# Grouped-query attention on one core: two q heads cast singly, and the copies of the keys' other half moved behind q's transposes

## The chip, the core and the metric

The kernel runs on one core of a Trainium2 chip. The core has a matrix engine (TensorE, PE in the rows), a vector engine (VectorE, DVE), an activation engine (ScalarE, ACT), a general engine (GpSimd, POOL) and an engine that issues transfers (SyncE, SP). Each takes its own list of instructions in order, and they wait for one another by semaphores. Transfers (DMAs) run on 16 DMA engines of the core. The metric is the device time of one execution in microseconds (us); the time shown of the kernel before is the median of three runs.

## The reference

```python
batch, n_q_heads, n_kv_heads, seq, head_dim = (8, 8, 2, 1024, 64)
...
for g in range(n_kv_heads):
    q_group = q[:, q_start:q_end, :, :].copy()
    k_group = k[:, g:g + 1, :, :].copy()
    v_group = v[:, g:g + 1, :, :].copy()
    scores = scale * np.matmul(q_group, k_group.transpose(0, 1, 3, 2))
    scores_max = np.max(scores, axis=-1, keepdims=True)
    attn = np.exp(scores - scores_max)
    attn = attn / (np.sum(attn, axis=-1, keepdims=True) + 1e-08)
    output[:, q_start:q_end, :, :] = np.matmul(attn, v_group)
```

Inputs and output are float32. There are 8 batches of 8 q heads, 64 heads in all (0 to 63 below), and 16 key and value tiles, each shared by four consecutive q heads.

## The kernel before, in words

**Tiles.** The scores of one head are computed transposed, in eight tiles: a score tile holds 128 keys against 512 queries, twice, for the two halves of the queries. One tile is a pair of matmuls (L400), which read `qt` (a head of q, turned) and `kt` (a key tile, turned). There are 512 score tiles. Each is turned into weights by ScalarE (`pt`, an exponential, L411) or by VectorE and GpSimd together (`ye` and `zz`, L422, L431, L448, L457, L463: an exponential made from the bits of a float). PE then multiplies the weights by the values `va` (L491) into `ops`, with a column of ones for the sums; VectorE takes the reciprocal (L560) and scales the result (L571) into `ost`, which SyncE stores (L378).

**Loads of q and k.** Head 0 and key tile 0 are turned on PE at the start. Every other head goes this way: GpSimd issues a DMA that casts float32 to bfloat16 into a buffer in DRAM (`qd`, L174, called from `cast_q`), most of them two heads at a time; SyncE then issues a DMA that turns a head on its way into `qt` (L243, `turn_q`). A key tile goes the same way by `kd` and `kt` (L233, `turn_k`). Such a turned tile holds the even sequence rows in partitions 0 to 63 and the odd ones in 64 to 127. Two more DMAs (`copy_k`) write the other half of `kt`, the same data with the partition halves exchanged, for the score tiles 4 to 7 of each head:

```python
nc.sync.dma_start(out=t[D : 2 * D, 1, :], in_=t[0:D, 0, :])
nc.sync.dma_start(out=t[0:D, 1, :], in_=t[D : 2 * D, 0, :])
```

Both read what the transpose of the key tile wrote, so the first of them waits on SyncE until that has landed, and everything behind it on SyncE's list waits too. The rows call them L237 and L238.

**The order.** The string `ORDER` sets the order of the whole program by hand; each letter appends instructions to the lists of their engines. `A` is a score tile for ScalarE, `a` to `g` one for VectorE, `x` and `p` are their exponentials, `V` some weighted sums. `X4`, `X6`, `X8` cast heads of q (`q10` and on do the same later), `Y` and `k` cast key tiles, `Z` and `v` values; `T` turns the next head, `K` the next key tile, `C` makes its two copies, `U` loads values, `S` stores a head, `G` is a product on GpSimd. A cast by `X`, `Y` or `Z` is also made to wait for the score tile that stands last before it in the string (L348). In the rows of the order below, `qd_171` and its like are the cast heads; the number only tells one buffer from another.

Of the kernel before, what the change touches and what calls it, by code (L numbers as in the profile page):

```python
# [25 lines left out]
VVVG0,108nxd2A0TpVSVVxVVVVA1zd2xA0TG1,148pVVVVVxVVVVA1Crnd2xA0pVSVVVVxVG0,36VVVA1zk2e2xA0pVVVG1,47VV
xVVVVVA1zq16d2xA0t3VVVVVG2,115rVxVpVA1VVVVxVVVnA0d2m2xVSVG1,71VpA1TVVxVVVVA0t2e2xG1,78pA1VVVVVxUVVA0
rze2TxVVG2,107VKpA1VVxVVVVVnA0A2xzq18VSVVVVVt3Ve1xA0G2,84pTVVVVVxVVVA2rzd1xA0G3,172pVVVVVxVVVVVA2nCe
1xA0pVVVVVVxVVVA2v2rt3A1xVVVm2VVVVVVVxe0A2G1,192pVVVxVVVVTA1ne0xA2pVSVVVVxVVVVA1rt2e0q20xA2pVVVG1,47
VVxVVVVA1m1G0,106e0nxA2pVSVVVVxUVVVA1ze0xA2G1,78pVVVVVxVVVA1rze0xA2G2,72pVVVVxVVVTA1t3e0xVG1,192VpA2  # L30
VVVxVVA1ne0xVVpVSA2VVVxVVVrA1m1q22A0t2xVVVVVt1VTVVVxVVG0,32nd2A1zVSVxVVG1,71A0pVVVxVVKVVA1zd2xA0G2,7
8rpVVVVVxVVVVA1zd2xA0G3,75pTVVVVVxVVVA1nG2,18A2xVzVk3VSVVVVVt4Vxd0A1G3,191rpTVCVVVxVVVVA2ne0xA1pVSVV
VVVxVVVA2m2q24A0xVVVVVVVrVt2xVVVVA1G3,30nd2xA0m3G1,71pSTVVVVVxVVVA1t3d2xA0G1,79pVVVVVxVVA1rzA2xVVVm2
VVVVVG1,106nd0xUA1pVVVVVxVVVVA2m1q26A0xVVKVt2VVTVVVVxVt1d1A2G0,72pVVxVVVA0VVzxVv3VVVA1Tzd2xA0G2,184r
pVVVVVxVVVVA1nd2xA0pSVVVVCVxVVVVrA1t2d2xA0G1,71pVVVVVxVVVVzA1q28A2xVzVVVVVG3,114nd0xA1pVSVVVxVVVVA2r
Tm3A0xG2,30VnVVVVVt3Se1xA2G2,71pVVVVVxVVVA0m2e1xA2G1,78pTVVVVVxVUVVA0rt2d1xA2G1,178pVVVVxVVVVA0nTd1x
A2pSVVVVVxVVVA0q30zA1xVzVVVVVVVrG2,106nxd2A0pVVSVVxVVVVA1t3d2xA0KG2,71pVVVVVxVVVA1ze2xA0G3,79pVVVVVx
VVVA1rTzA2k4xVVt4VVVVVVG3,115xne0A1pVSVVxVVA2VVrCVxm3Vq32VVVA0m2A1xVVVVVVVTVVG1,106nxe2A0pVSVVVxVVVV
VA1Tt3d2xA0G1,78pVVVVVVxVVVA1rt2A2xVVVm1VVVVG0,107nd0xA1pVVVVVxVVVVA2t1d0xVG0,78VpTA1VVVxVUVVA2rzA0x
VVq34zVVVVVVnxe1G2,71A2pVSVVVxVVKVVA0G1,10rne1G1,98xA2pVVSVVVxVVVVA0t2v4e1xA2pTVVG1,47VVVxVVVA0ze1xA  # L40
2G2,78pVVVVVxVVVA0rm2G1,106e1CnxA2pTVSVVVxVVVVA0t2e1xA2G1,71pVVVVVxVVVA0m1q36A1zxVVVVVG1,122VrVnVxd2
A0pSVVVVxVVVVA1t2e2xA0G1,71pVVVVVxVVVVA1ze2xA0G2,63pVVVVVVxVUVVVTzA1e2xG2,78rA0pVVVVVVxVVVA1t3A2xVzV
VVVTVVVG3,114ne0xA1pVSVVVxVVVKVA2rm3A0q38xzVVVVVVt4e1xA2G3,225pVVVVVxVVVTA0nd1xA2rpSVVVVVxVVVVA0ne1x
A2m3G2,71SpVVVCVVxVVVVA0t3k5A1xVVm2VVVVe2xG1,78A0rpVVVVVxVVVVA1zq40A2xVVzVVVVVVG3,106ne0xA1pVTVVVVxV
VVVA2t4e0xA1G3,72pVVVVVxVVVVVA2rG2,105ne0xA1pSVVVVVVxVUVVVm2A2e0xA1G1,78pVVVVVVxVVVA2rTt3d0xVVVG1,71
pA1VVVxVVVVzA2q42A0xVzVKVVVVG3,107nd1xA2pTVSVVVVxVVVA0t4d1xA2G2,78rpVTVVVVxVVVA0t3v5d1xA2pVG2,82VVVV
xVVVA0nA1CxVm2VVSVVTVzVd2xA0G2,191rpVVVVVxVVVVA1nd2xA0pSVVVVVxVVVVt3A1q44e2xm2A0G1,70VpVVVVxVVVVA1t2
e2xA0G1,78pVVVVVxVVVVA1rm1e2xA0G0,228pVVVVVxVVUVVTA1ne2xA0rSpVVVVVxVVVA1nA2xVm0VVSt1VVTVVVVxt0VA0A1q
46zVxVVVzVVVVVVxVzd2A0G2,114rpVVxVVVVKA1VVxnVVVVA2m2Sd0xA1G1,71pVVVVVxVVVVt2A2Te0xG1,114rA1pVVVVVxVV
VVA2nA0xVzk6VVVVVVVzCe1xA2G3,71pVVVVVxVVVVVA0Trq48t3e1xA2pVVG2,90VVVVxVVVVA0nA1xVm1VVSVVVd2xA0G2,71T  # L50
pVVVVxVVVVA1m2e2xG0,78A0rpVVVVVxVVVA1t2e2xG0,107A0pVVVVVxVUVVA1nA2xVzVVSVVVVt2Ve0xA1G1,71rpVVVVxVVVV
VA2q50ze0xA1pTVVG1,204VVVxVVVA2ne0xA1rpSVVVVVxVVVA2nA0xVzv6VSVVVVt3e1xA2KG2,52pVVVVVxVVVVA0ze1xA2G2,
71pVVVVVxVVVVA0t3Td1xVG2,185VrVpA2VVxVVVVTA0ne1xA2pSVVVVCVxVVVA0q52zA1xVVzVVVVVVrVG3,106nxd2A0pVSVVV
xVVVVA1t4d2xA0G3,71pVVVVVxVVVVTA1m3A2xrVt3VVVVVVG2,108Vne0xA1pVSVVVVxVVVVA2ze0xA1G3,78pVVVVVxVVVUVA2
rzA0q54xVVVVm4VTVG3,108Vne1xKA2pVVVVxVVVVA0t4d1xA2G3,71pVVVVVxVVVTzA0e1xG4,77rA2pVVVVVxVVVA0nG3,24A1
xzVk7VSVVVCVt5d2xA0G4,71pVVTVVxVVVVA1m4q56A2xVVVrVt4Ve0xG3,202A1pVVVVVxVVVVA2nd0xA1pSVVVVVxVVVA2rm3e
0G2,106nxVVA1pSVVVxVVVVA2t3e0xA1G2,71pVVVVVUxVA2m2xze0A1TTt3xA2G2,71pVVVxVVVVVA1zq58A0xVVm3VVVVVVe2x
G2,199A1rKpVVVVVxVVVVA0nd2xA1pSVVVVVVxVVVA0Tm2v7A2t3xVVVVVt2VVVxd1G1,200A0rpVVVVxVVVVVA2nCe1xA0pSVVV
VVVxVVVVzA2Te1xG2,56rA0pVVVVVVxVVG1,45VA2nA1xVzq60VVSVVVVVt3e0xA2G2,78pVVVVVxVVVVVA1rm2e0xA2G1,184pV
VVVVxVVVA1ne0xA2pSVTVVVxVUVVA1t2A0xVVm1VVVVzVe2xA1G1,194rpVVVVxVVVVA0ne2xA1pVVVTVVxVVVVm1q62A0t2d2xA  # L60
1G0,75pVVVVVVxVVVA0rt1d2xA1G0,181pVVKVVVxVVVA0ne2xA1pSVVVVxVVVA0zq63A2TxVVzVVVVVVt2xe1A0G1,199rpVVVx
VVVVVA2ne1xCA0pVSVVVVxVVVVVrA2m1e1G0,106nxA0VVpVVSVVVxVVVVA2Tt1d1xA0G0,71pVVVVVVxVVVVA2TzA1xVVm1VVVV
VrVt1Vxe0A2G0,185pVVVVxVVVVVA1ne0xA2pSVVVVVVxVVVUVA1zd0xA2G1,71rpVVVVVVxVVVVA1zA0xVVt2VVVVVVG1,106nd
2xA1pVSVVVVxVVVVA0ze2xA1G2,71pVVVVVxVVVA0m2A2rxVt2VVVVVG1,112Vnxe1A0pSVVVVxVVVVVA2zd1xA0G2,114rpVVVV
VVVxVVVA2nA1xVm2VVSzVVVVVVxVt3VVA0A2m1xVVVVVVVVVm2xVVVA1A0xVVrVt2VVVVVxVnVVA2rt1A1xVVVzVVVVVVxTnVVVV
# [30 lines left out]
def kernel(  # L96
# [76 lines left out]
    def cast(src, t):  # L173
        return nc.gpsimd.dma_start(  # L174
            out=t.rearrange("(a x) d -> a (x d)", a=128),
            in_=src.rearrange("(a x) d -> a (x d)", a=128),
        )
# [429 lines left out]
```

## Time and profile before

| what | value |
|---|---|
| median of 3 runs | 356.24 us (356.08 to 357.02) |
| the profiled execution's own time | 354.45 us |
| its span, first to last instruction | 352.7 us |
| PE, DVE, ACT, POOL busy, share of the span | 97%, 97%, 96%, 82% |
| chain that ended last | PE 58%, ACT 25%, DVE 7%, DMA 5% |
| mean granted clock of PE | 0.990 |

Rows of a timeline read: start, length, engine, line, operation, written tile `<-` read tiles, shape, count, and in brackets the idle time of the engine just before and what ended it. `SPq` is SyncE's list; its rows give the time that the issue of a DMA took, not the transfer. The time to landing runs from the issue to the end of the transfer. The clock column of the windows table is the share of full speed that was granted to PE.

### The profile page before, as it was taken

Reading aid. Unit: us, or ns where it says so; the run is one execution under the profiler, and the core shown is the slowest. Engines: PE = TensorE matmul, PEld = TensorE weight load, DVE = VectorE, ACT = ScalarE, POOL = GpSimd, SP = SyncE. Lnnn points to the kernel's source line nnn. Section 1 sums busy time; section 2 is a strip of 40 time slices with the busy share of each in tenths; the row PEclk is TensorE's granted clock in tenths of the full one; section 3 lists DMA queues with packets and bytes.
Section 4 is the critical chain, followed back from the end, with each engine's and each line's share of the span. In section 5 each row is a group of like instructions: output and inputs, shape, how many; then the busy total and the mean of one; then the engine's idle time right before and its main releaser. Section 6 shows DMA issues by size and latency. Waiting matters only on the chain.

```text
span 352.7 us, 14190 instructions
## 1 busy us (share of the span) xinstructions
PE 341.2 (97%) x6268; PEld 225.7 (64%) x6268; DVE 342.3 (97%) x518; ACT 340.1 (96%) x370; POOL 287.9 (82%) x235
## 2 busy tenths in 40 slices
PE   7879999999999999999999999999999999999995
PEld 3445665666666666666666676766665666676774
DVE  5979999999999999999999999999999999999996
ACT  6959999999999999999999999999999999999994
POOL 3447989999988999998999989899998989987000
PEclk9979999999999999999999999999999999999999
DMA  6986677675787588677668979576876653623123
GB/s 149 141 160 122 127 134 160 137 121 110 134 159 126 126 153 128 122 149 148 121 121 122 165 153 136 98 162 113 156 138 134 140 122 80 134 63 88 51 82 103
DMA packets 96574, 44.84 MB, mean 127 GB/s; under 512 B 61168, under 2 KB 95344, under 8 KB 95728
## 3 DMA queue, kind: packets, MB, share of 16 engines
q1 hardware_dynamic: 94128, 31.34, 40.3%
q0 software_dynamic: 2096, 12.19, 24.0%
q8 instruction: 49, 0.80, 1.0%
q10 hardware_dynamic: 288, 0.39, 0.3%
q14 instruction: 13, 0.11, 0.1%
HBM read 27.13 MB, written 28.97 MB: 159 GB/s over the span
## 4 chain that ended last, share of the span: by engine, by line
PE 58%; ACT 25%; DVE 7%; DMA 5%; issue 2%; SPq 1%; POOL 0%; DVEq 0%
PE ops L491 32%; PE sp L400 25%; ACT pt L411 25%; DVE ye L422 3%; DMA kt<-kd 2%; DMA qt<-qd 1%; DMA vs<-in_v_dram 1%; DMA kd<-in_k_dram 1%; DVE ye L463 1%; DVE ost L571 1%; DVE zz L431 1%; PE sp L529 1%; DVE zz L457 0%; SPq L238 0%; DVE rec L560 0%
## 5 line engine op out<-in xcount | busy, mean ns | idle before, releaser
L411 ACT ACTIVATE pt<-sp 128x1024 bf16<-128x1024 f32 x366 | 337.5, 1049 | 5.0 <-PE sp L400 4.9
L448 POOL TENSOR_TENSOR zz<-ye,zz 128x568 bf16<-128x568 bf16 (+29 forms) x126 | 248.4, 1973 | 27.8 <-DVE rec L560 8.7
L422 DVE TENSOR_SCALAR ye<-sp 128x1024 uint16<-128x1024 f32 x146 | 177.3, 1214 | 2.4 <-PE sp L400 2.0
L400 PE MATMUL sp<-qt,kt 64*128 64x512 bf16 x1024 | 167.2, 384 | 6.2 <-ACT pt L411 2.6
L491 PE MATMUL ops<-va,pt 128*128 128x65 bf16 x2832 | 161.9, 195 | 0.0
L491 PEld LDWEIGHTS <-pt 128*128 128x128 bf16 x2832 | 121.4, 98 | 31.4 <-issue 31.4
L491 PE MATMUL ops<-va,zz 128*128 128x65 bf16 x1136 | 123.7, 194 | 0.0
L491 PE MATMUL ops<-va,ye 128*128 128x65 bf16 x1104 | 119.5, 194 | 0.0
L491 PEld LDWEIGHTS <-ye 128*128 128x128 bf16 x1104 | 83.8, 98 | 15.7 <-issue 14.8
L491 PEld LDWEIGHTS <-zz 128*128 128x128 bf16 x1136 | 86.4, 98 | 9.2 <-issue 8.9
L400 PEld LDWEIGHTS <-kt 64*128 64x128 bf16 x1024 | 51.2, 93 | 61.7 <-issue 38.1
L431 DVE TENSOR_SCALAR zz<-ye 128x2048 uint16<-128x2048 uint16 (+1 forms) x77 | 51.9, 686 | 0.1
L463 DVE TENSOR_SCALAR ye<-ye 128x2048 uint16<-128x2048 uint16 (+1 forms) x77 | 49.9, 655 | 0.0
L571 DVE TENSOR_TENSOR ost<-ops,rec 128x448 f32<-128x448 f32 (+2 forms) x73 | 44.5, 610 | 0.3
L457 DVE TENSOR_TENSOR zz<-ye,zz 128x2048 bf16<-128x2048 bf16 (+31 forms) x54 | 33.5, 625 | 0.0
L174 POOL DMA_DIRECT2D qd<-in_q_dram x33 | 23.3, 706 | 5.5 <-PE sp L400 4.7
L560 DVE RECIPROCAL rec<-ops 128x7 f32<-128x7 f32 (+2 forms) x73 | 14.4, 197 | 0.8 <-PE ops L491 0.8
L443 POOL MEMSET tick<- 128x1 bf16 x52 | 9.7, 186 | 0.0
L174 POOL DMA_DIRECT2D kd<-in_k_dram x8 | 5.8, 719 | 0.1
L174 POOL DMA_DIRECT2D vd<-in_v_dram x8 | 5.6, 701 | 0.0
L269 PE MATMUL ops<-warm 128*128 128x512 bf16 (+1 forms) x12 | 3.6, 448 | 1.2 <-DVE warm L168 1.2
L529 PEld LDWEIGHTS <-pt 128*128 128x128 bf16 x96 | 3.4, 98 | 1.2 <-issue 1.2
(37 smaller groups left out, 26.1 us busy)
## 6 DMA issues: line engine op xcount, KB each, us to landing
out_dram<-ost SPq DMA_DIRECT2D x63, 256.0 KB, 3.2
qd<-in_q_dram POOLq DMA_DIRECT2D x29, 256.0 KB, 4.5
kt<-kt SPq DMA_DIRECT2D x30, 64.0 KB, 4.5
va<-vd SPq DMA_DIRECT2D x30, 64.0 KB, 3.1
kd<-in_k_dram POOLq DMA_DIRECT2D x7, 256.0 KB, 4.5
vd<-in_v_dram POOLq DMA_DIRECT2D x7, 256.0 KB, 5.2
qt<-qd SPq DMA_TRANSPOSE x63, 4.2
qd<-in_q_dram POOLq DMA_DIRECT2D x5, 128.0 KB, 3.9
```

What stands on the lines that cost most here:

```text
L174: return nc.gpsimd.dma_start(out=t.rearrange("(a x) d -> a (x d)", a=128), in_=src.rearrange("(a x) d -> a (x d)", a=128),)
L400: now = nc.tensor.matmul(sps[x][:, hf, :], lhsT=t[lo : lo + D, c // NH, ci % NH * 128 : (ci % NH + 1) * 128], rhs=qt[j][lo : lo + D, 0, :] ...
L411: exps.append(nc.scalar.activation(out=p, in_=where_s[(j, c)], func=AF.Exp, scale=scale))
L422: vec = nc.vector.tensor_scalar(out=ye[:, i, :, :], in0=where_s[(j, c)], scalar1=EXP_A, scalar2=EXP_B, op0=ALU.mult, op1=ALU.add,)
L431: vec = nc.vector.tensor_scalar(out=ch.tiles(zz), in0=ch.tiles(ye), scalar1=0x7F, scalar2=0x3F00, op0=ALU.bitwise_and, op1=ALU.bitwise_or,)
L443: tock = nc.gpsimd.memset(tick, 0.0) if any(old) else None
L448: gps = nc.gpsimd.tensor_tensor(out=z, in0=flat(ch.tiles(ye))[:, ch.cols : ch.cols + w], in1=z, op=ALU.mult)
L457: vec = nc.vector.tensor_tensor(out=z, in0=flat(ch.tiles(ye))[:, 0 : ch.cols], in1=z, op=ALU.mult)
L463: vec = nc.vector.tensor_scalar(out=ch.tiles(ye), in0=ch.tiles(ye), scalar1=0x7F80, scalar2=None, op0=ALU.bitwise_and,)
L491: ended[job] = nc.tensor.matmul(ops[g % 2][:, lo : lo + D + 1], lhsT=p[:, par, qs * 128 : (qs + 1) * 128], rhs=va[(b * G + h // HPG) % NVA ...
L560: vec = nc.vector.reciprocal(out=to, in_=sums)
L571: vec = nc.vector.tensor_tensor(out=to, in0=src, in1=by, op=ALU.mult)
```

## The change

In `cast_q`, heads are cast in pairs from head 6 on instead of head 4 on. In `ORDER`, `X4` stands earlier and casts head 4 alone, `X5` is new and casts head 5 alone at about the place where `X6` stood, and `X6` and `X8` (heads 6 and 7, heads 8 and 9) stand later. The first `C` moves behind three `T`, and each of the other fourteen `C` also stands later, behind other instructions of SyncE's list. Some `T` move by a few letters. No instruction of PE, ScalarE or VectorE changes its place.

```diff
-A0IX3TY1a1xA2pxA0za1xKA2pE0E2TxFA0m0E3xA1za2t1E5X4FxpFA0E1xm0A1X6E6zxb2t1A0pE7E4xA1Crzxb2nG0,78A0pxA
-1TTY2m1xb2A0G0,50pxA1X8t1Z1xA2zb0VVVt1VxVVG0,78VpA1TVVxVVVVrA2zc0G1,101xnVVpA1SVVxVVVVVKA2rm1A0xG0,3
...
+A0IX3TY1a1xA2pxA0za1xKA2pX4E0E2TxFA0m0E3xA1za2t1E5FxpFA0E1xm0A1E6X5zxb2t1A0pE7E4xTA1rzxb2nG0,78A0pxX
+6A1Y2m1xb2A0G0,50pxA1Tt1Z1xA2zb0VVVt1VxVVG0,78VpA1VVxVVVVrA2zc0TG1,101xnVVCpA1SVVxVVVVX8VKA2rm1A0xG0
...
-        n = 2 if 3 < j < NJ - 2 else 1
+        n = 2 if 5 < j < NJ - 2 else 1
```

SyncE's list at the start, from the transpose of key tile 1 (`kd_1_175`) and of head 3 (`qd_171`) on:

```order
 L233 DMA_TRANSPOSE kt<-kd_1_175 128x1x512
 L243 DMA_TRANSPOSE qt<-qd_171 128x1x512
+L243 DMA_TRANSPOSE qt<-qd_203 128x1x512
+L243 DMA_TRANSPOSE qt<-qd_296 128x1x512
+L243 DMA_TRANSPOSE qt<-qd_356 128x1x512
 L237 DMA kt<-kt 64x512
 L238 DMA kt<-kt 64x512
-L243 DMA_TRANSPOSE qt<-qd_256 128x1x512 x2
-L243 DMA_TRANSPOSE qt<-qd_288 128x1x512
 L378 DMA out_dram<-ost 128x512
```

The transposes of heads 4 (`qd_203`), 5 (`qd_296`) and 6 (`qd_356`), which stood behind the two copies of key tile 1, now stand ahead of them.

GpSimd's list at the same time, from the casts of head 3 and of key tile 1 on:

```order
 L174 DMA qd_171<-in_q_dram 16x4096
 L174 DMA kd_1_175<-in_k_dram 16x4096
-L174 DMA qd_256<-in_q_dram 16x8192
-L174 DMA qd_288<-in_q_dram 16x8192
-L448 TENSOR_TENSOR zz<-ye,zz 128x624
-L174 DMA kd_0_363<-in_k_dram 16x8192
+L174 DMA qd_203<-in_q_dram 16x4096
+L174 DMA qd_296<-in_q_dram 16x4096
+L448 TENSOR_TENSOR zz<-ye,zz 128x624
+L174 DMA qd_356<-in_q_dram 16x8192
+L174 DMA kd_0_361<-in_k_dram 16x8192
 L448 TENSOR_TENSOR zz<-ye,zz 128x400
```

The cast of heads 4 and 5 together (16x8192) became two casts of one head each (16x4096), and the cast of heads 6 and 7 moved from before the first product to behind it, ahead of the cast of key tiles 2 and 3.

SyncE's list further on, from the transpose of key tile 4 (`kd2_0_1182`) on, first before, with the numbers of the tiles:

```order
L233 DMA_TRANSPOSE kt_1397<-kd2_0_1182 128x1x512
L378 DMA out_0_dram<-ost_92 128x4x128
L243 DMA_TRANSPOSE qt_1471<-qd16_1227 128x1x512
L237 DMA kt_1397<-kt_1397 64x512
L238 DMA kt_1397<-kt_1397 64x512
L243 DMA_TRANSPOSE qt_1663<-qd16_1227 128x1x512
```

and the same stretch of the changed kernel:

```order
L233 DMA_TRANSPOSE kt_1397<-kd2_0_1182 128x1x512
L378 DMA out_0_dram<-ost_92 128x4x128
L243 DMA_TRANSPOSE qt_1471<-qd16_1227 128x1x512
L237 DMA kt_980<-kt_980 64x512
L238 DMA kt_980<-kt_980 64x512
L243 DMA_TRANSPOSE qt_1663<-qd16_1227 128x1x512
```

Where the copies of key tile 4 (`kt_1397`) stood, behind the transpose of head 16, now stand those of key tile 3 (`kt_980`), which stood behind the transpose of head 13 before.

More of the change, by code (lines that the diff above doesn't have):

```diff
@@ L20 @@
 ORDER = """
-A0IX3TY1a1xA2pxA0za1xKA2pE0E2TxFA0m0E3xA1za2t1E5X4FxpFA0E1xm0A1X6E6zxb2t1A0pE7E4xA1Crzxb2nG0,78A0pxA
-1TTY2m1xb2A0G0,50pxA1X8t1Z1xA2zb0VVVt1VxVVG0,78VpA1TVVxVVVVrA2zc0G1,101xnVVpA1SVVxVVVVVKA2rm1A0xG0,3
-1nVVb1t1v1UxA2pVG0,46VVVVxVVVVA0m0TTq10c1zxA2VpVG0,56VVVVxVVVVA0t1c1xzA2G1,200pVVVVCVVxVVVVA0rnc1xA2
-VpSVVVVxVVVVA0zc1xA2G1,71pVVVVVxVVVTTVA0t2q12c1xA2pVVG1,57VVVxVVVVA0rzd1xA2G1,191pVVVVVxVVVA0nd1xA2p
-SVVVVxVVUVA0rm1d1xt2VVVG0,71pA2VVxVVVA0t1q14c1xVpA2TG0,167VVVxVVA0ne1xVKpVSA2VVVxVVVrA0m0zA1xVVt1VVV
@@ L26 @@
[L26 to L65, printed above, removed]
@@ L66 @@
-A0m0A2SxVVVVVVVVm1VVxVVVA1A0xVrVt1VVVVVVVVt0xA2A1nVVVVxVzVVSVVVVV+1VxA0A2VVVVxVm0VVVVVVVVVVxVVVrt0A1
-A0xVnVVVVVV+0VVVSVxVA2b1VrVxVpVVVA0VVxVVVnVA2a1zxSVVpVA0VVxVVVVVm0A2A1xzVVVVrVVm0VVVVxVVVnVA0A2t1xSV
-t0VVL1,1+1L3,1L4,1xL5,1+0L6,1L0,1rnL2,1L7,1Srn
+A0IX3TY1a1xA2pxA0za1xKA2pX4E0E2TxFA0m0E3xA1za2t1E5FxpFA0E1xm0A1E6X5zxb2t1A0pE7E4xTA1rzxb2nG0,78A0pxX
+6A1Y2m1xb2A0G0,50pxA1Tt1Z1xA2zb0VVVt1VxVVG0,78VpA1VVxVVVVrA2zc0TG1,101xnVVCpA1SVVxVVVVX8VKA2rm1A0xG0
+,31nVVb1t1v1UxA2pVG0,46VVVVxVVVVA0m0Tq10c1zxA2VpVG0,56VVVVxVVVVA0t1Tc1xzA2G1,200pVVVVVVxVVVVA0rnc1xA
@@ new lines @@
+2VpSVVVVxVVVVA0zc1xA2G1,71pVVVVVxVVVTTVA0t2q12c1xA2pVVG1,57VVVxVVVVA0rzd1xA2G1,191pVVVVVxVVVA0nd1xA2
+pSVVVVxVVUVA0rm1d1xt2VVVG0,71pA2VCVxVVVA0t1q14c1xVpA2TG0,167VVVxVVA0ne1xVKpVSA2VVVxVVVrA0m0zA1xVVt1V
+VVVVVG0,108nxd2A0TpVSVVxVVVVA1zd2xA0TG1,148pVVVVVxVVVVA1rnd2xA0pVSVVVVxVG0,36VVVA1zk2e2xA0pVVVG1,47V
+VxVVVVVA1zq16d2xA0t3VVVVVG2,115rVxVpVA1VVVVxVVVnA0d2m2xVSVG1,71VpA1TVVxVVVVA0t2e2xG1,78pA1VVVVVxUVVA
+0rze2TxVVG2,107VKpA1VVxVVVVVnA0A2xzq18VSVVVVVt3Ve1xA0G2,84pTVVVVCVxVVVA2rzd1xA0G3,172pVVVVVxVVVVVA2n
@@ new lines @@
+e1xA0pVVVVVVxVVVA2v2rt3A1xVVVm2VVVVVVVxe0A2G1,192pVVVxVVVVTA1ne0xA2pVSVVVVxVVVVA1rt2e0q20xA2pVVVG1,4
+7VVxVVVVA1m1G0,106e0nxA2pVSVVVVxUVVVA1ze0xA2G1,78pVVVVVxVVVA1rze0xA2G2,72pVVVVxVVVTA1t3e0xVG1,192VpA
+2VVVxVVA1ne0xVVpVSA2VVCVxVVVrA1m1q22A0t2xVVVVVt1VTVVVxVVG0,32nd2A1zVSVxVVG1,71A0pVVVxVVKVVA1zd2xA0G2
+,78rpVVVVVxVVVVA1zd2xA0G3,75pTVVVVVxVVVA1nG2,18A2xVzVk3VSVVVVVt4Vxd0A1G3,191rpTVVVVxVVVVA2ne0xA1pVSV
+VVVVxVVVA2m2q24A0xVVVVVVVrVt2xVVVVA1G3,30nd2xA0m3G1,71pSTVVVVVxVVVA1t3d2xA0G1,79pVVVVVxVVA1rzA2xVVVm
@@ new lines @@
+2VVVVVG1,106nd0xUA1pVVVVVxVVCVVA2m1q26A0xVVKVt2VVTVVVVxVt1d1A2G0,72pVVxVVVA0VVzxVv3VVVA1Tzd2xA0G2,18
+4rpVVVVVxVVVVA1nd2xA0pSVVVVVxVVVVrA1t2d2xA0G1,71pVVVVVxVVVVzA1q28A2xVzVVVVVG3,114nd0xA1pVSVVVxVVVVA2
+rTm3A0xG2,30VnVVVVVt3Se1xA2G2,71pVVVVVxVVVA0m2e1xA2G1,78pTVVVVVxVUVVA0rt2d1xA2G1,178pVVVVxVVVVA0nTd1
+xA2pSVVVVVxVVVA0q30zA1CxVzVVVVVVVrG2,106nxd2A0pVVSVVxVVVVA1t3d2xA0KG2,71pVVVVVxVVVA1ze2xA0G3,79pVVVV
+VxVVVA1rTzA2k4xVVt4VVVVVVG3,115xne0A1pVSVVxVVA2VVrVxm3Vq32VVVA0m2A1xVVVVVVVTVVG1,106nxe2A0pVSVVVxVVV
@@ new lines @@
+VVA1Tt3d2xA0G1,78pVVVVVVxVVVA1rt2A2xVVVm1VVVVG0,107nd0xA1pVVVVVxVVVVA2t1d0xVG0,78VpTA1VVVxVUVVA2rzA0
+xVVq34zVVVVVVnxe1G2,71A2pVSVVVxVVKVVA0CG1,10rne1G1,98xA2pVVSVVVxVVVVA0t2v4e1xA2pTVVG1,47VVVxVVVA0ze1
+xA2G2,78pVVVVVxVVVA0rm2G1,106e1nxA2pTVSVVVxVVVVA0t2e1xA2G1,71pVVVVVxVVVA0m1q36A1zxVVVVVG1,122VrVnVxd
+2A0pSVVVVxVVVVA1t2e2xA0G1,71pVVVVVxVVVVA1ze2xA0G2,63pVVVVVVxVUVVVTzA1e2xG2,78rA0pVVVVVVxVVVA1t3A2xVz
+VVVVTVVVG3,114ne0xA1pVSVVVxVVVKVA2rm3A0q38xzVVVVVVt4e1CxA2G3,225pVVVVVxVVVTA0nd1xA2rpSVVVVVxVVVVA0ne
@@ new lines @@
+1xA2m3G2,71SpVVVVVxVVVVA0t3k5A1xVVm2VVVVe2xG1,78A0rpVVVVVxVVVVA1zq40A2xVVzVVVVVVG3,106ne0xA1pVTVVVVx
+VVVVA2t4e0xA1G3,72pVVVVVxVVVVVA2rG2,105ne0xA1pSVVVVVVxVUVVVm2A2e0xA1G1,78pVVVVVVxVVVA2rTt3d0xVVVG1,7
+1pA1VVVxVVVVzA2q42A0xVzVKVVVCVG3,107nd1xA2pTVSVVVVxVVVA0t4d1xA2G2,78rpVTVVVVxVVVA0t3v5d1xA2pVG2,82VV
+VVxVVVA0nA1xVm2VVSVVTVzVd2xA0G2,191rpVVVVVxVVVVA1nd2xA0pSVVVVVxVVVVt3A1q44e2xm2A0G1,70VpVVVVxVVVVA1t
+2e2xA0G1,78pVVVVVxVVVVA1rm1e2xA0G0,228pVVVVVxVVUVVTA1ne2xA0rSpVVVVVxVVVA1nA2xVm0VVSt1VVTVVVVxt0VA0A1
@@ new lines @@
+q46zVxVVVzVVVVVVxVzd2A0G2,114rpVVxVVVVKA1CVVxnVVVVA2m2Sd0xA1G1,71pVVVVVxVVVVt2A2Te0xG1,114rA1pVVVVVx
+VVVVA2nA0xVzk6VVVVVVVze1xA2G3,71pVVVVVxVVVVVA0Trq48t3e1xA2pVVG2,90VVVVxVVVVA0nA1xVm1VVSVVVd2xA0G2,71
+TpVVVVxVVVVA1m2e2xG0,78A0rpVVVVVxVVVA1t2e2xG0,107A0pVVVVVxVUVVA1nA2xVzVVSVVVVt2Ve0xA1G1,71rpVVVVxVVV
+VVA2q50ze0xA1pTVVG1,204VVVxVVVA2ne0xA1rpSVCVVVVxVVVA2nA0xVzv6VSVVVVt3e1xA2KG2,52pVVVVVxVVVVA0ze1xA2G
+2,71pVVVVVxVVVVA0t3Td1xVG2,185VrVpA2VVxVVVVTA0ne1xA2pSVVVVVxVVVA0q52zA1xVVzVVVVVVrVG3,106nxd2A0pVSVV
@@ new lines @@
+VxVVVVA1t4d2xA0G3,71pVVVVVxVVVVTA1m3A2xrVt3VVVVVVG2,108Vne0xA1pVSVVVVxVVVVA2ze0xA1G3,78pVVVVVxVVVUVA
+2rzA0q54xVVVVm4VTVG3,108Vne1xKA2pVVCVVxVVVVA0t4d1xA2G3,71pVVVVVxVVVTzA0e1xG4,77rA2pVVVVVxVVVA0nG3,24
+A1xzVk7VSVVVVt5d2xA0G4,71pVVTVVxVVVVA1m4q56A2xVVVrVt4Ve0xG3,202A1pVVVVVxVVVVA2nd0xA1pSVVVVVxVVVA2rm3
+e0G2,106nxVVA1pSVVVxVVVVA2t3e0xA1G2,71pVVVVVUxVA2m2xze0A1TTt3xA2G2,71pVVVxVVVVVA1zq58A0xVVm3VVVVVVe2
+xG2,199A1rKpVVVVVxVVVVA0nd2CxA1pSVVVVVVxVVVA0Tm2v7A2t3xVVVVVt2VVVxd1G1,200A0rpVVVVxVVVVVA2ne1xA0pSVV
@@ new lines @@
+VVVVxVVVVzA2Te1xG2,56rA0pVVVVVVxVVG1,45VA2nA1xVzq60VVSVVVVVt3e0xA2G2,78pVVVVVxVVVVVA1rm2e0xA2G1,184p
+VVVVVxVVVA1ne0xA2pSVTVVVxVUVVA1t2A0xVVm1VVVVzVe2xA1G1,194rpVVVVxVVVVA0ne2xA1pVVVTVVxVVVVm1q62A0t2d2x
+A1G0,75pVVVVVVxVVVCA0rt1d2xA1G0,181pVVKVVVxVVVA0ne2xA1pSVVVVxVVVA0zq63A2TxVVzVVVVVVt2xe1A0G1,199rpVV
+VxVVVVVA2ne1xA0pVSVVVVxVVVVVrA2m1e1G0,106nxA0VVpVVSVVVxVVVVA2Tt1d1xA0G0,71pVVVVVVxVVVVA2TzA1xVVm1VVV
+VVrVt1Vxe0A2G0,185pVVVVxVVVVVA1ne0xA2pSVVVVVVxVVVUVA1zd0xA2G1,71rpVVVVVVxVVVVA1zA0CxVVt2VVVVVVG1,106
@@ L69 @@
+nd2xA1pVSVVVVxVVVVA0ze2xA1G2,71pVVVVVxVVVA0m2A2rxVt2VVVVVG1,112Vnxe1A0pSVVVVxVVVVVA2zd1xA0G2,114rpVV
+VVVVVxVVVA2nA1xVm2VVSzVVVVVVxVt3VVA0A2m1xVVVVVVVVVm2xVVVA1A0xVVrVt2VVVVVxVnVVA2rt1A1xVVVzVVVVVVxTnVV
+VVA0m0A2SxVVVVVVVVm1VVxVVVA1A0xVrVt1VVVVVVVVt0xA2A1nVVVVxVzVVSVVVVV+1VxA0A2VVVVxVm0VVVVVVVVVVxVVVrt0
+A1A0xVnVVVVVV+0VVVSVxVA2b1VrVxVpVVVA0VVxVVVnVA2a1zxSVVpVA0VVxVVVVVm0A2A1xzVVVVrVVm0VVVVxVVVnVA0A2t1x
+SVt0VVL1,1+1L3,1L4,1xL5,1+0L6,1L0,1rnL2,1L7,1Srn
 """
```

## The prediction

> **What bounds the kernel now.** I read the stretches of the span first, then the chain that ended last, and then the timelines of the engines where that chain leaves them. In the windows table the steady part is full: from 30 to 130 us three engines are each busy over 99 us of 100, so time won there would have to come off all three.
>
> ```profile
> 21.20:24.61 3.41, 0.99 (x14) 0.45 (x12) 1.59 (x3) 1.28 (x2) 0.94 (x1) 1.00 0.95 185
> 24.61:28.03 3.42, 3.42 (x39) 1.92 (x37) 2.63 (x5) 1.74 (x2) 1.14 (x2) 0.50 0.52 131
> ...
> 30.00:130.00 100.00, 99.48 (x1831) 65.36 (x1828) 99.64 (x147) 99.86 (x110) 92.87 (x68) 1.00 0.71 134
> ```
>
> Columns: stretch, its length, busy PE, PEld, DVE, ACT and POOL, granted clock, DMA share, GB/s. The loose stretch is 21.2 to 28.0: PE works 0.99 of 3.41 us, and then 3.42 us at half the granted clock. The chain of waits (start, length, what) says why.
>
> ```profile
> 10.72 6.31 DMA kt<-kd
> 17.69 1.34 SPq L238
> 19.13 4.90 DMA qt<-qd
> ...
> 27.31 8.28 ACT pt L411 x9
> ```
>
> Before 24 us the end hangs on SyncE: the transpose of the second key tile, then the issue of that tile's second copy, then the transpose of a q head. PE's timeline has the same place.
>
> ```profile
> 21.35 0.39 PE L400 MATMUL sp<-qt,kt 64*128 64x512 bf16 x2
> 24.16 0.39 PE L400 MATMUL sp<-qt,kt 64*128 64x512 bf16 x2 [2.42 <-DMA qt<-qd]
> ```
>
> Counted in program order, the pair at 24.16 is the 25th score tile, the first of head 4. It waits 2.42 us for head 4's transpose. SyncE's queue shows what stood in front of it.
>
> ```profile
> 10.72 1.13 SPq L233 DMA_TRANSPOSE kt<-kd  x1
> 11.89 2.44 SPq L243 DMA_TRANSPOSE qt<-qd  x1
> 17.11 0.54 SPq L237 DMA_DIRECT2D kt<-kt  x1
> ...
> 19.13 4.24 SPq L243 DMA_TRANSPOSE qt<-qd  x3
> 23.46 0.54 SPq L378 DMA_DIRECT2D out_dram<-ost  x1
> ```
>
> The copy at L237 needs the key transpose, which landed at 10.72 + 6.31 = 17.03. From 14.33 (11.89 + 2.44) to 17.11 SyncE does nothing but wait for it, then spends until 19.1 on two copies; only then is head 4 transposed.
>
> **The change part by part.** *Head 4's path.* The copies go behind three transposes, and the cast of head 4 no longer waits for a later score tile or carries head 5. The old casts and their neighbours on GpSimd:
>
> ```profile
> 10.46 0.49 POOL L174 DMA_DIRECT2D qd<-in_q_dram  x1 [3.11 <-PE sp L400]
> 12.25 0.62 POOL L174 DMA_DIRECT2D qd<-in_q_dram  x1 [1.30 <-PE sp L400]
> 14.45 1.36 POOL L448 TENSOR_TENSOR zz<-ye,zz 128x624 bf16<-128x624 bf16 x1 [1.58 <-DVE zz L431]
> 15.91 0.55 POOL L174 DMA_DIRECT2D kd<-in_k_dram  x1
> 16.48 0.95 POOL L448 TENSOR_TENSOR zz<-ye,zz 128x400 bf16<-128x400 bf16 x1
> 17.74 0.85 POOL L174 DMA_DIRECT2D qd<-in_q_dram  x1 [0.31 <-PE sp L400]
> ```
>
> ```profile
> 6.97 1.31 PE L400 MATMUL sp<-qt,kt 64*128 64x512 bf16 x6 [0.63 <-ACT pt L411]
> ```
>
> The new gate of head 4's cast is the sixth score tile, the last of the run at 6.97, over at 8.28. Landing times of the DMAs concerned (count, KB, median us to landing):
>
> ```profile
> qd<-in_q_dram POOLq DMA_DIRECT2D x5, 128.0 KB, 3.9
> ```
>
> ```profile
> qd<-in_q_dram POOLq DMA_DIRECT2D x2, 256.0 KB, 4.8
> kt<-kd SPq DMA_TRANSPOSE x1, 6.3
> qt<-qd SPq DMA_TRANSPOSE x1, 5.7
> ```
>
> So head 4's cast lands at about 8.3 + 3.9 = 12.2, not 10.46 + 4.8 = 15.3. Its transpose is issued when head 3's issue is over, 14.33. With the 4.9 us it takes now it lands at 19.2; with the 6.3 of the slowest in that crowd, at 20.6. PE wants it when the tile before is done, at 21.74 (21.35 + 0.39). I take 19.2 to 20.6: the wait of 2.42 us goes entirely, with 1.1 us of cover left at the worse end.
>
> *What that is worth.* The two engines behind PE show their idle time there.
>
> ```profile
> 25.51 1.02 ACT L411 ACTIVATE pt<-sp 128x1024 bf16<-128x1024 f32 x1 [2.70 <-PE sp L400]
> 27.31 4.69 ACT L411 ACTIVATE pt<-sp 128x1024 bf16<-128x1024 f32 x5 [0.78 <-PE sp L400]
> ```
>
> ```profile
> 24.59 1.23 DVE L422 TENSOR_SCALAR ye<-sp 128x1024 uint16<-128x1024 f32 x1 [1.82 <-PE sp L400]
> 26.61 0.20 DVE L560 RECIPROCAL rec<-ops 128x7 f32<-128x7 f32 x1 [0.79 <-PE ops L491]
> ...
> 28.51 1.23 DVE L422 TENSOR_SCALAR ye<-sp 128x1024 uint16<-128x1024 f32 x1 [0.21 <-PE sp L400]
> ```
>
> ScalarE can come forward by 2.70 + 0.78 = 3.48, VectorE by 1.82 + 0.79 + 0.21 = 2.82. Afterwards both are over 99% busy, so the engine with the smaller lead decides, and I take 2.8. The lower end is 1.8, the stall alone as VectorE sees it; the upper end 3.5, if ScalarE's share counts.
>
> The 0.79 and 0.21 are the price of the half clock from 24.61 to 28.03. Their loss belongs to the stall only if the stall brought the clock down, and the rows say so: the stretch before has 0.99 us of PE work in 3.41 and is followed by 0.50. The Trainium skill (TensorE: Matmul & The Clock Gate, "Why this matters for your kernels") asks for no idle gap over about 3 us and lets the clock fall after a whole idle window. By that rule a wait of 2.42 us would not cost the clock and the gain would be 1.8; this trace disagrees, and the measurement decides.
>
> *The casts.* One cast more is issued, 0.49 us of GpSimd, where GpSimd now waits 3.11 and 1.30 us for PE; without that cover it would cost 0.5. Head 5's cast takes the place of the cast at 12.25, half as large. The cast of heads 6 and 7 now follows the product at 14.45, so the key cast and the next product are 0.55 us later; a product that ended at 17.43 (16.48 + 0.95) ends at 18.0, and PE's weighted sums, the first that could read it, start only here:
>
> ```profile
> 18.51 0.24 PE L491 MATMUL ops<-va,ye 128*128 128x65 bf16 x1
> ```
>
> The 0.5 us between hide the delay; uncovered it costs 0.5. Head 6's transpose then waits for its cast, 15.9 + 4.8 = 20.7, where it stood at about 21.8 before. Nothing is lost there.
>
> *The copies of the second key tile* come after it, about 22 to 24, landing by 30 at the longest landing below. They are wanted by the 40th score tile, 35.15 before, about 32.3 when all else is 2.8 sooner: hidden by some 2 us. The casts of heads 8 and 9 wait for the 26th tile, about 22.5, instead of the cast at 17.74: they land at about 28.1, and SyncE reaches the transpose of head 8 at about 28.8, as now.
>
> ```profile
> qt<-qd SPq DMA_TRANSPOSE x1, 6.4
> ```
>
> ```profile
> 27.50 2.64 SPq L243 DMA_TRANSPOSE qt<-qd  x2
> ...
> 38.89 0.97 PE L400 MATMUL sp<-qt,kt 64*128 64x512 bf16 x6
> ```
>
> Head 8 is the second of that pair, landed at 28.8 + 6.4 = 35.2, and its first tile is among the three from 38.89. With a lead of 2.8 it is wanted at 36.1. This is what is late next: 0.9 us of cover, and each us beyond is paid.
>
> *The copies of the other fourteen key tiles* move by some 9 to 19 us, by where the instruction now ahead of each stands, and cost the same issues, 0.53 and 0.59 us. The least room is at the fourth key tile: SyncE is through with the transpose ahead of them at 69.57 (67.41 + 2.16), and the half that they fill is wanted at 79.48.
>
> ```profile
> 67.41 2.16 SPq L243 DMA_TRANSPOSE qt<-qd  x1
> ```
>
> ```profile
> 79.48 0.60 PE L400 MATMUL sp<-qt,kt 64*128 64x512 bf16 x4
> ```
>
> ```profile
> DMA to landing us min/median/max: 2.0/4.6/6.6
> ```
>
> That leaves 9.91 - 1.12 - 6.6 = 2.2 us even with the longest landing of any key transfer. I put the body at nothing, with 0 to +0.5 for transposes that now stand 1.1 us later.
>
> *The sum.* Profiled execution 354.45 (span 352.7), less 2.8: about 351.6. The three timed runs have a median of 356.24, 1.8 above it; I take the difference of 2.8 over to that median: **353.4 us**.
>
> **The rivals.** *The transpose is late anyway.* The DMA share is 0.95 around the stall, and a transpose in the crowd took 6.3. For: head 4's transpose now runs beside the casts of heads 5, 6 and 7. Against: these carry less in that stretch than two casts of 256 KB did, and the copies are gone. It decides from a landing after 21.74, a flight over 7.4 us; at 23 the gain is 1.8 - 1.3 = 0.5 plus part of the clock, about 355.4. The Trainium skill (DMA: Bandwidth & Descriptors, "Queues, rings and completion order") says that each DMA engine goes round between queues packet by packet, so that a place ahead in SyncE's queue is no place ahead of GpSimd's casts; no row contradicts it, and it is the mechanism of this rival.
>
> *The stall moves to head 8.* For: only 0.9 us of cover and a cast with a later gate. Against: with the casts after it sooner, less should stand beside it than the 6.4 shows. If it lands 2 us later, 1.1 is given back, and up to 1.8 with a half clock behind it: 355.0.
>
> *Slower: copies late in the body.* SyncE stands behind stores that wait for VectorE; the longest such wait is 4.9 us.
>
> ```profile
> SPq L378 <- DVE zz L457: 11.9, 6, 4.9
> ```
>
> Where such a wait falls before a moved copy beyond what the old timeline shows, the 2.2 us are used up and PE waits for the excess, up to 2.7, at the first tile of the second half. One group would cost less than is won; it takes two full ones, or five at 1 us, to turn the sum: about 358. Against: the room at the other groups is 0.7 to 5 us larger, and the stores' waits are already in the 69.57.
>
> **How the numbers follow.** No change means within 0.3%, 355.2 to 357.3, about what these runs can tell. The forecast has 0.73, own range 352.4 to 354.6 (gains of 3.8 to 1.6); late transpose 0.10, two in five of it faster; head 8 0.12, half of it faster; slower 0.05. Faster: 0.73 + 0.04 + 0.06 = 0.83; slower 0.05; same the rest, 0.12. The range reaches from a gain of 3.9, ScalarE's lead and a little, to 355.6, into the rivals.
>
> **What would show it.** Right: PE's wait for a q transpose at the 25th tile is gone, ScalarE's idle time of 2.70 and VectorE's 1.82 with it, no half clock after 24.6, SyncE issuing head 4's transpose near 14.3 and the copies near 22 to 24. Wrong: a wait at L400 for a transpose at the 25th or 47th tile, or for a copy at the first tile of a second half; a clock of 0.5 that stays; or all of it as said and the later stretches longer by what was won.

## The result, and the profile after

| | before | changed |
|---|---|---|
| median of the timed runs | 356.24 us (353.28 to 357.02, 8 runs) | 352.75 us (351.01 to 353.56, 8 runs) |
| the profiled execution's own time | 354.45 us | 352.72 us |
| its span | 352.7 us | 350.9 us |

The ratio of the times is 0.9905, with a 95% interval of 0.9875 to 0.9934: the change makes the kernel 3.5 us (1.0%) faster. The forecast was 353.4, a gain of 2.8. The ratios, here and below, leave out single executions more than 1.5% above the fastest of the same kernel, which the medians and spreads include.

PE's timeline after the change, at the place of the old wait:

```profile
20.40 0.60 PE L400 MATMUL sp<-qt,kt 64*128 64x512 bf16 x4
...
25.71 0.20 PE L491 MATMUL ops<-va,ye 128*128 128x65 bf16 x1 [1.31 <-DVE ye L463]
```

The second pair of the run at 20.40 is the 25th score tile, head 4's first; no wait stands ahead of it, where 2.42 us stood. SyncE's list of the same execution, and the time to landing of head 4's transpose:

```profile
14.52 1.46 SPq L243 DMA_TRANSPOSE qt<-qd  x1
```

```profile
12.10 9.14 SPq L243 DMA_TRANSPOSE qt<-qd  x4
21.33 0.78 SPq L237 DMA_DIRECT2D kt<-kt  x1
22.17 0.58 SPq L238 DMA_DIRECT2D kt<-kt  x1
22.84 1.04 SPq L378 DMA_DIRECT2D out_dram<-ost  x1
```

```profile
qt<-qd SPq DMA_TRANSPOSE x1, 2.9
```

Four transposes are issued in a row, head 4's at 14.52 (it was 19.13), and it lands at 17.4. The copies follow at 21.33.

Then a new wait appears: the 1.31 us at 25.71, for a step of VectorE at L463. VectorE's and GpSimd's timelines show where it comes from.

```profile
20.53 0.43 DVE L431 TENSOR_SCALAR zz<-ye 128x1024 uint16<-128x1024 uint16 x1
...
23.33 2.33 DVE L463 TENSOR_SCALAR ye<-ye 128x2048 uint16<-128x2048 uint16 x1
```

```profile
22.46 0.55 POOL L174 DMA_DIRECT2D qd<-in_q_dram  x1
23.03 0.66 POOL L448 TENSOR_TENSOR zz<-ye,zz 128x248 bf16<-128x248 bf16 x1
23.64 0.55 POOL L174 DMA_DIRECT2D vd<-in_v_dram  x1
24.20 0.89 POOL L448 TENSOR_TENSOR zz<-ye,zz 128x368 bf16<-128x368 bf16 x1
```

The step of 2048 columns at L463 takes 2.33 us, where the same shape took 0.69 at 27.61 before. GpSimd's product of 248 columns runs when the step begins, and the step ends 0.56 us after the product of 368 columns does. In the kernel before another step had been held in this way, and the change freed it (0.43 above):

```profile
20.00 2.43 DVE L431 TENSOR_SCALAR zz<-ye 128x1024 uint16<-128x1024 uint16 x1
```

```profile
19.09 3.05 POOL L448 TENSOR_TENSOR zz<-ye,zz 128x624 bf16<-128x624 bf16 x2
```

This hold is no chance of one execution: the two other runs below that leave head 4's cast and key tile 1's copies in the old order have it as well (2.42 us each), and no run with either moved has it.

The start times of score tiles (rows of L400) in the two profiles show the sum of it:

| score tile | before, us | changed, us | sooner by |
|---|---|---|---|
| 23rd | 19.78 | 19.42 | 0.36 |
| 25th (head 4) | 24.16 | 20.63 | 3.53 |
| 29th | 28.08 | 23.12 | 4.96 |
| 35th | 31.80 | 29.92 | 1.88 |
| 47th (head 8) | 39.12 | 37.32 | 1.80 |
| 512th | 345.84 | 344.06 | 1.78 |

The lead grows to 5 us, falls to 1.9 within the six tiles after the held step, and is then carried to the end without change. Of the 3.53 us at the 25th tile, 0.36 were there at the 23rd and 2.42 are the wait. The other 0.75 are PE's work between these two tiles, 1.96 us before and 1.21 in the changed kernel: up to 21.20 it ran at an earlier half clock, which the prediction did not count. Whether the change removed it is not shown: two of the runs below with the changed casts and copies have a half clock at that place too (from 17.70 and 18.13).

```profile
17.79:21.20 3.41, 3.41 (x44) 2.26 (x42) 3.41 (x6) 2.73 (x4) 3.40 (x4) 0.50 0.72 112
```

A half clock takes part in the fall of the lead too; the windows of the changed kernel (columns as in the prediction):

```profile
16.17:19.58 3.41, 2.65 (x33) 1.26 (x32) 3.41 (x7) 3.41 (x5) 3.37 (x6) 1.00 0.75 121
19.58:22.99 3.41, 3.41 (x62) 2.20 (x61) 3.41 (x8) 3.41 (x5) 3.33 (x3) 1.00 0.94 198
22.99:26.41 3.42, 1.78 (x35) 1.09 (x32) 3.42 (x3) 2.64 (x3) 2.72 (x5) 1.00 0.88 163
26.41:29.82 3.41, 3.41 (x42) 2.14 (x40) 3.13 (x6) 1.94 (x2) 1.56 (x2) 0.50 1.45 210
```

### The profile page after: what moved, and what is told of

It reads as the page before. It is cut to its first block, busy times and chain, and to the rows that moved or that the text cites. A ratio compares the mean times of both kernels' runs of the same rounds, so it can differ in the third digit from the quotient of the medians.

```text
span 350.9 us, 14187 instructions
## 1 busy us (share of the span) xinstructions
PE 340.2 (97%) x6268; PEld 225.7 (64%) x6268; DVE 342.1 (97%) x518; ACT 339.8 (97%) x370; POOL 288.6 (82%) x236
## 4 chain that ended last, share of the span: by engine, by line
PE 55%; DVE 30%; ACT 8%; issue 3%; DMA 2%; SPq 0%; DVEq 0%
PE ops L491 30%; PE sp L400 24%; DVE ye L422 15%; ACT pt L411 8%; DVE ye L463 4%; DVE zz L431 4%; DVE ost L571 3%; DVE zz L457 3%; DMA kt<-kd 2%; DVE rec L560 1%; PE ops L269 1%; PE sp L529 1%; PE sp L292 0%; DVE kt L313 0%; PE ops L304 0%
## 5 line engine op out<-in xcount | busy, mean ns | idle before, releaser
L400 PE MATMUL sp<-qt,kt 64*128 64x512 bf16 x1024 | 166.5, 383 | 4.3 <-ACT pt L411 3.0
L400 PEld LDWEIGHTS <-kt 64*128 64x128 bf16 x1024 | 51.6, 93 | 58.9 <-issue 34.9
L463 DVE TENSOR_SCALAR ye<-ye 128x2048 uint16<-128x2048 uint16 (+1 forms) x77 | 51.6, 676 | 0.0
L431 DVE TENSOR_SCALAR zz<-ye 128x2048 uint16<-128x2048 uint16 (+1 forms) x77 | 49.7, 657 | 0.1
L174 POOL DMA_DIRECT2D qd<-in_q_dram x34 | 23.7, 697 | 5.6 <-PE sp L400 4.6
```

The lines of the kernel that those rows point to most:

```text
L174: return nc.gpsimd.dma_start(out=t.rearrange("(a x) d -> a (x d)", a=128), in_=src.rearrange("(a x) d -> a (x d)", a=128),)
L400: now = nc.tensor.matmul(sps[x][:, hf, :], lhsT=t[lo : lo + D, c // NH, ci % NH * 128 : (ci % NH + 1) * 128], rhs=qt[j][lo : lo + D, 0, :] ...
L431: vec = nc.vector.tensor_scalar(out=ch.tiles(zz), in0=ch.tiles(ye), scalar1=0x7F, scalar2=0x3F00, op0=ALU.bitwise_and, op1=ALU.bitwise_or,)
L463: vec = nc.vector.tensor_scalar(out=ch.tiles(ye), in0=ch.tiles(ye), scalar1=0x7F80, scalar2=None, op0=ALU.bitwise_and,)
```

## The experiments

Two theories were to be told apart first: head 4 was late because SyncE waited for the copies, or because its cast was late.

**Only the first copies moved.**

```diff
-...xA1Crzxb2nG0,78...TVVxVVVVrA2zc0...
+...xA1rzxb2nG0,78...TCVVxVVVVrA2zc0...
```

> The kernel before, with one edit: the two copies of key tile 1 stand behind the transposes of heads 4, 5 and 6 in SyncE's list; all casts and the other fourteen pairs of copies as before. Theory (head 4 is late because SyncE waits for the copies): its transpose is issued when its pair cast has landed, about 15.3, lands near 20 to 20.7, the wait of 2.42 us at the 25th score tile is gone, and the time is that of the full change within 0.5 us, 352.3 to 353.3. Rival (the cast is what is late, so the smaller and sooner cast does it): the wait stays over 1 us, and the time is over 355.

Measured: 352.10 us, ratio 0.9904 (0.9882 to 0.9925). Head 4's transpose was issued at 14.42 and took 7.8 us, so it landed at 22.2 and not by 20.7; no wait is left at the 25th tile, but one of 0.82 us at the 22nd, for head 3. The theory holds for the wait and, to 0.2 us, for the time: this edit alone, on its median, has the gain of the whole change. The profile is of the longest of its six runs (353.33 us), with 6.8 us of half clock from 18.4 on; that execution gained 1.1 us on the profile of before, so the profile does not show where the median's gain comes from.

**Only the casts changed**, the copies all back in their old places (the reverse of the diff's moves of `C`, in the changed kernel).

> The changed kernel, with all fifteen pairs of copies put back where they stood in the kernel before: only the casts of heads 4 to 9 and the places of some transposes are changed. Theory (the copies ahead are the cause): head 4's transpose is again issued behind the copies, at 18 to 19.1, and lands at 22.5 to 24; a wait of 1 to 2.4 us stays at the 25th score tile, and the time is 355 to 356.3. Rival (the sooner cast is the cause): no wait, and 352.3 to 353.3.

Measured: 352.78 us, ratio 0.9921 (0.9895 to 0.9947). SyncE's timeline and PE's, of this run:

```profile
15.55 0.54 SPq L237 DMA_DIRECT2D kt<-kt  x1
16.13 0.58 SPq L238 DMA_DIRECT2D kt<-kt  x1
16.82 1.31 SPq L243 DMA_TRANSPOSE qt<-qd  x1
```

```profile
23.02 0.39 PE L400 MATMUL sp<-qt,kt 64*128 64x512 bf16 x2 [1.07 <-DMA qt<-qd]
```

Both theories were wrong on this run in part: the wait stays, at 1.07 us, as the first said, and the time is the one that the second gave. The copies are still ahead of head 4, but the key transpose that they wait for took 4.2 us instead of 6.3, so they are issued at 15.55 instead of 17.11. That goes with the casts: the nine profiles with the new casts have 4.0 to 4.7 us for this transpose, the three with the old ones 5.9 to 6.3. This run also has neither of the two held VectorE steps: L463 took 0.68. The two halves of the change are two remedies for one stall; on the medians either is enough, and their gains do not add.

**Only the later fourteen pairs of copies moved**, in the kernel before.

> The kernel before, with only the fourteen later pairs of copies moved as in the change; the copies of key tile 1 and all casts stay as before. Theory (the later moves are hidden): 356.2, within 0.5 us of the kernel before, no wait at the first score tile of a second half. Rival (they give or cost something by themselves): over 1 us from it in either direction, with a wait or a lost wait at such a tile after 50 us.

Measured: 355.64 us, ratio 0.9997 (0.9982 to 1.0013). The later moves do nothing, as expected. The start of this kernel has the same instructions in the same order as the kernel before, and its profile shows how far the old stall varies, 3.79 us here:

```profile
24.32 0.61 PE L400 MATMUL sp<-qt,kt 64*128 64x512 bf16 x2 [3.79 <-DMA qt<-qd]
```

**The cast of heads 8 and 9 behind the product**, in the changed kernel: where the lead of 5 us went.

```diff
-...VVVVX8VKA2rm1A0xG0,31nVV...
+...VVVVVKA2rm1A0xG0,31X8nVV...
```

> The changed kernel, with one edit: the cast of heads 8 and 9 stands behind the small product of GpSimd (128x248) instead of ahead of it. Theory (the lead of 4.9 us at 23 us is given back because that cast, 0.55 us of GpSimd, pushes the product into VectorE's step at L463, which then took 2.33 instead of 0.69 us): the product ends near 23.1, ahead of the step at 23.3, the step takes 0.7 us, PE's wait of 1.31 us for it is gone, and the time is 1 to 2 us below the changed kernel, 350.7 to 351.8. Rival (the step is held by the issue of the casts on GpSimd and not by the products, or the lead is lost to PE's half clock whatever VectorE does): the step stays over 1.5 us, or the time stays within 0.5 us of 352.75.

Measured: 351.02 us, ratio 0.9872 (0.9851 to 0.9893). VectorE's step of this run, and then PE's:

```profile
23.53 0.68 DVE L463 TENSOR_SCALAR ye<-ye 128x2048 uint16<-128x2048 uint16 x1
```

```profile
36.68 0.61 PE L400 MATMUL sp<-qt,kt 64*128 64x512 bf16 x4 [1.51 <-DMA qt<-qd]
```

The step is no longer held, and the lead of 4.2 us lasts to the 46th tile. There 1.7 us of it goes, at the first tile of head 8: the wait that the prediction named as the next one. Time and step came as the theory said.

**Head 7 turned sooner**, so that head 8 is issued sooner.

```diff
-...c0TG1,101...A0m0Tq10c1...
+...c0TTG1,101...A0m0q10c1...
```

> The run with the cast of heads 8 and 9 behind the product, with one more edit: the transpose of head 7 stands directly behind that of head 6, ahead of the copies of key tile 1. That run lost 1.7 us of its lead of 4.2 us at the 47th score tile, the first of head 8, whose transpose was issued behind head 7's at 30.8 us and landed 5.7 us later. Theory (head 8 is late next because SyncE issues it late): it is issued when its cast has landed, about 29, lands near 34.5, the wait of 1.51 us shrinks below 0.5, and the time is 0.8 to 1.7 us below that run's 351.0, 349.3 to 350.2. Rival (the DMA engines are the bound there): the transpose takes over 6.5 us, the wait stays over 1 us, 350.7 to 351.3.

Measured: 351.98 us, ratio 0.9913 (0.9886 to 0.9940). Head 8's transpose was issued at 28.67 and took 8.1 us; PE waited 2.21 us for it. The twelve runs spread from 350.75 to 356.48 us, and the median is above the ranges of both theories. The theory falls: head 8 was issued 2.1 us sooner and landed no sooner (36.8, after 36.5), so the transfer, and not its place in SyncE's list, makes head 8 late. Counted in the order string, head 7, which is transposed ahead of it in both runs, is first wanted at the 62nd tile and head 8 at the 47th; to transpose head 8 first was not tried.

**The cast of heads 6 and 7 later**, in the kernel before: whether fewer bytes beside the key transpose were what helped the casts-only run.

```diff
-...A1X6E6zx...A0pxA1TTY2...
+...A1E6zx...A0pxX6A1TTY2...
```

> The kernel before, with one edit: the cast of heads 6 and 7 stands behind GpSimd's first product, as in the change, instead of ahead of it; heads 4 and 5 are still cast together, and all copies stand as before, key tile 1's ahead of head 4's transpose. Theory (with the casts alone, the gain came from fewer bytes in flight while key tile 1 is turned, so that the copies stop holding SyncE sooner): key tile 1 lands in 4 to 5 us instead of 6.3, the copies are issued near 15.7, head 4's transpose near 17, the wait at the 25th score tile is under 1.3 us, and the time is 352.3 to 354. Rival (the sooner, smaller cast of head 4 is needed): the key transpose still takes over 5.7 us, and the time is within 1 us of the kernel before.

Measured: 357.09 us in the median of twelve runs from 352.14 to 358.81 us (before on that chip: 355.82), ratio 0.9998 (0.9963 to 1.0032): unclear. The profile is of the longest of these, so it shows a mechanism and not a typical size. The key transpose landed at 16.8, 5.2 us after its issue, between what the two theories said; head 4's was issued at 18.12, a us sooner than before, and then took 9.2 us:

```profile
27.44 0.61 PE L400 MATMUL sp<-qt,kt 64*128 64x512 bf16 x2 [6.50 <-DMA qt<-qd]
```

I read it so: what was taken from beside one transpose was put beside the next, and the gain needs the smaller, sooner cast of head 4 as well. One profile does not show that.

**Two cast issues between the products**, in the changed kernel: whether products alone hold VectorE, or cast issues too.

```diff
-...VG0,46VVVVxVVVVA0m0Tq10c1...
+...Vq10G0,46VVVVxVVVVA0m0Tc1...
```

> The changed kernel, with one edit: the cast of heads 10 and 11 stands ahead of GpSimd's product of 368 columns, so that two cast issues and no product follow the product of 248 columns. It tells what held VectorE's step at L463 for 2.33 us. Theory (products alone hold it): it starts when the product of 248 ends and takes 1.0 to 1.2 us. Rival (cast issues hold it as well): it ends behind the two issues, 1.8 us or longer.

Measured: 356.47 us in one run, and nothing on its question: VectorE had waited 1.05 us for PE at 21.96, the step at L463 came 0.9 us later beside the product and was not held at all (0.69). Head 7's transpose took 10.1 us, head 8's 6.8, and PE waited 2.92 us for head 8. The cast of heads 10 and 11, at 25.00 instead of 25.03, now follows hard behind two others, but one run does not show that this is why: without the edit, a second profile of the change (below) has 9.7 us for head 7 and 5.4 for head 8.

**The cast of heads 10 and 11 later**, on top of head 7 turned sooner.

```diff
-...A0m0q10c1zxA2...c1xzA2G1,200...
+...A0m0c1zxA2...c1xzA2q10G1,200...
```

> The run with head 7 turned sooner, with one more edit: the cast of heads 10 and 11 stands behind the product of 448 columns, about 2 us later, so that it is not in flight while head 8 is turned. Theory (head 8 then lands under 5.5 us after its issue): no wait at the 47th score tile, and 349.0 to 350.0. Rival (heads 10 and 11 become late, first wanted at the 59th tile): a wait for a transpose between the 55th and 65th tile, and 350.5 to 351.5.

Measured: 351.09 us, ratio 0.9865 (0.9836 to 0.9893). Head 8's transpose took 6.2 us, not under 5.5, and PE waited 0.40 us. The expected end of the wait came nearly; the time is 1.1 us above the range and inside the rival's, though the rival's wait between the 55th and 65th tile did not come. It is not to be told from the run with the one edit (351.02).

**The change and the two better kernels on one chip.**

> The changed kernel once more, beside the two better ones on one chip. Theory (the cast of heads 8 and 9 and the product behind it hold VectorE's step at L463 in the change's own order, in every execution): the step takes over 2 us again at about 23 us, and the median is 1 to 2 us over those of the other two. Rival (the hold was a chance of one execution): the step takes 0.7 us, and the medians differ by under 0.5 us.

Measured: 352.44 us (352.24 to 352.82), ratio 0.9916 (0.9892 to 0.9940). The step was held again:

```profile
23.04 2.35 DVE L463 TENSOR_SCALAR ye<-ye 128x2048 uint16<-128x2048 uint16 x1
```

Head 4's transpose differs between the two profiles of this one kernel: here it was issued at 15.04, took 4.9 us and landed at 19.98, 0.3 us before PE's 25th tile at 20.31.

> The changed kernel with the cast of heads 8 and 9 behind the product, once more. Theory: 350.5 to 351.5, 1 to 2 us below the change; the step at L463 takes 0.7 us. Rival: within 0.5 us of the change.

Measured: 351.44 us, ratio 0.9894 (0.9866 to 0.9923); the step took 0.68 us. PE did not wait for head 8 in this execution, though the lead at the 46th tile was 3.4 us: its transpose was issued at 28.40 and landed at 35.1, and PE came to it at 35.78.

> The same with head 7 turned sooner and the cast of heads 10 and 11 later, once more. Theory (head 8 is what is late next, and its transpose is slow where that cast is in flight): under 0.6 us of wait at the 47th score tile, 350.4 to 351.2, 0 to 0.7 us below the run with one edit. Rival (it is no better): above it by over 0.3 us.

Measured: 350.88 us, ratio 0.9872 (0.9846 to 0.9898), with 0.5 us of wait at head 8. The order of the three medians is the one expected, but the intervals overlap. The last is the best seen: by the medians 5.2 us below the kernel before on that chip (356.04) and 1.6 us below the change.

## Why the prediction was right, point by point

**Head 4's path held.** Issue was forecast for 14.33 and came at 14.52; landing for 19.2 to 20.6, and it came at 17.4, because the transpose took 2.9 us and not 4.9 to 6.3. The wait of 2.42 us went entirely, with 3 us of cover and not 1.1. The large cover was luck. In the second profile of the change the transpose took 4.9 us, as I had forecast, and landed at 19.98. The cover there was 0.3 us, since PE, without the earlier half clock, came to the tile at 20.3 and not at the 21.74 that I had taken.

**The worth of it was mis-sized.** The term was the smaller of the two leads, VectorE's 2.82. The lead measured is 5.0 at the 29th tile and 1.8 at the end of the same two profiles, and 3.5 between the medians. That 2.8 lies between these is partly luck, as a gain and a loss that I had both left out work against each other. Three things were not in the term.

- VectorE's step at 20.00 held for 2.43 us stood in the timeline that I had read; I took it as part of the fixed work. It cost VectorE 2.0 us over its usual 0.43, and the change freed it. With it VectorE's lead is 2.82 + 2.00 = 4.82, about the 5.0 that the 29th tile shows.
- *The casts* was the step that failed. I costed the moved cast of heads 8 and 9 by when it lands, and its 0.55 us on GpSimd at nothing. It pushes the product of 248 columns into VectorE's step at L463, which loses 1.64 us (2.33 less 0.69). With that one cast behind the product the step took 0.68 or 0.69 us in all five profiles, and the medians are lower by 1.7 us in one comparison, of separate timings, and by 1.0 in the other, on one chip. The intervals of the ratios overlap in both.
- The sign said no half clock after 24.6. There is one, from 26.41: PE's wait for the held step and the gaps beside it leave 1.78 us of work in the 3.41 before. The price that I gave for the old half clock was thus not all won.

**The median moved more than the profiles did**, 3.5 against 1.7. The profiled execution of before was 1.8 us below its median, that of the change at its median. The wait for head 4 was 2.42 us in that profile and 3.79 in another with the same start, so I think that the typical execution of before had the longer wait. That is not shown: the timed runs hold no row for it, and the execution with 3.79 took 355.08 us, only 0.6 more, so the wait can be a part of the 1.8 at most.

**The body at nothing** was right: the lead is 1.80 us at the 47th tile and 1.78 at the 512th, and the later moves alone give 0.9997.

**The rivals.** The late transpose did not come with the change, but such flights are real: 6.1, 7.8 and 9.2 us with other arrangements of the same casts, the last two over the 7.4 at which I let it decide. The stall at head 8 did not come either, since the lead had shrunk to 1.8 before it; where the lead stayed at 4.2, PE waited 1.51 us there, and 2.21 and 2.92 in two others, but not at all in the second profile of the kernel that had the 1.51. Place and order were right; the wait does not come each time. Copies late in the body were not seen in any run.

**The rule on the clock** that I weighed against the trace, that of the Trainium skill (TensorE: Matmul & The Clock Gate, "Why this matters for your kernels"), lets the clock fall after a whole idle window. It is contradicted again, by the windows above and those below.

What held VectorE between 23.7, when the first product ended, and 25.0 stays open. A cast issue ran in the first half of that time and the second product in the other; the run that was to separate them missed the moment. In the five profiles with the cast of heads 8 and 9 behind the product the step came just ahead of a cast issue and was not held, and the issue took 0.77 us where it took 0.55 above; that makes the cast issue a suspect as well, and settles nothing.

## What to carry to other kernels

When a stall is removed, read which instructions of other engines the earlier work now meets: here a cast of 0.55 us in front of a small product cost 1.0 to 1.7 us by the medians, and a held step showed as one row with four times its usual length. Two edits that attack one stall from two sides should be tried one by one, since each may have the whole gain. And a place in a queue is worth its time only while the transfers are quick: head 4's transpose took 2.9 to 9.2 us in these runs, and 2.9 and 4.9 in two executions of one kernel.
